# Decoder-step MLP on one core: PSUM split three ways, product order, early factors, and DMA issue moved to GpSimd

## The chip, the cores and the metric

The kernel runs on one core of one Trainium2 chip. The metric is the device time of one execution in microseconds; the time of a kernel is the median of its runs.

## The reference

One layer of a decoder trunk on 1024 prompt tokens and 8 sample tokens, width 1024, all float32: a pooling mixer and gated linear attention, cross-attention into 256 memory tokens, an MLP of hidden width 4096, and a final RMSNorm. The change touches the MLP and what surrounds it:

```python
hf = _rmsnorm(x, norm_ffn_g)
a = jax.nn.relu(jnp.einsum('btd,df->btf', hf, w_up))      # 1024 -> 4096
x = x + jnp.einsum('btf,fd->btd', a * a, w_down)          # 4096 -> 1024
y = _rmsnorm(x, norm_final_g)
```

## The kernel before, in words

**Arithmetic.** Every float32 operand of a large product is split into a high and a low part of the matmul type, and three partial products are summed: high by high, high by low, low by high. A split is a cast on ScalarE (L157) and a subtraction on VectorE (L158). Both MLP products use a two-by-two scheme with seven products in place of eight, numbered "1" to "7". Tokens are cut into columns 0 to 511 (HA = 512) and 512 to 1031 (HB = 520).

**The up product** comes in three pieces. The attention part ends with `run(ATTN)` (L1184) and the remaining columns of the attention's output projection (`add_ctx`, L1004). Then `first_products(m)` (L1114) runs for m = 0 to 15: products "1" and "2", 12 matmuls of 512 columns each, whose activated sum (tile `c11`) is stored to `fd["2"][m]` in HBM. Then `other_products(m)` (L1127) runs for m = 0 to 15. I call one m of it a row. A row loads four weight blocks into one slot `w4` (L1131), combines them on VectorE (L1140 to L1143), reloads the row's `c11` as `b11` (L1135), and runs products "4", "6", "5", "7", "3" in this order through `product` (L1107): "4" is 12 matmuls of 512 columns, each other one 24 of 260. Product "7" goes on accumulating in the accumulator of "6", and "3" in that of "5". So VectorE must have read "6" (L1155) before "7" starts, and ScalarE must have read "5" (L1158) before "3" starts. After that come the sums L1160 to L1164, the squared ReLU (L1111, L1112), and five factors formed by VectorE (L1172 to L1181; three of them are written over `w4`) and stored to HBM by GpSimd (L1173 to L1182). One more is stored by ScalarE (L1169).

**The down product** goes through the numbers in the order "2", "3", "1", "6", "5", "4", "7". For each it loads eight factors of two hidden blocks (`factor`, L1239, load at L1243, then split), and for each of four output blocks two weight pieces (`down_w`, L1248, load at L1257), multiplies (`down_part`, L1275), and adds to the residual blocks `X`, which `x2_load` (L1321, load at L1326) brings from HBM. The factors of the next number are loaded while the present one is multiplied.

**Buffers.** `S` (L66) has 19 slots of about 8 KB per partition, one for any `slot(...)`. During the rows they hold the split operands of products "3" to "7" (two slots each, ten in all), `P1` (four slots, each of four rows; one comes free after rows 3, 7, 11 and 15), the `w4` of the rows under way, and the early factors "2" (one slot each, kept until the down product). `tmp` (L68) has four buffers; a row takes two (`c12` with `b11`, and `c2`), a factor's raw load one. PSUM has eight banks: pool `mp` with two accumulators of one bank, `accp` with two of three banks (NG = 3). The down product opens pools of its own, with two of one bank and three of two banks.

**Order of the work.** The framework's scheduler puts the instructions of each engine in order ahead of time by the program's order and by when it expects operands and buffers; on the chip each engine, and each engine's DMA issue queue, then goes strictly in that order. A slot is taken when the DMA that read it last has landed. `first_factor` (L1201, load at L1206) is called after rows 2, 4, 5, 9 and 13; the remaining three factors "2" are loaded ahead of the down product's first weights, in program order. All loads of the MLP (L1131, L1135, L1206, L1243, L1257, L1326) are issued by SyncE (SP).

Of the kernel before, what the change touches and what calls it, by code (L numbers as in the profile page):

```python
# [8 lines left out]
F32 = mybir.dt.float32  # L9
# [51 lines left out]
def body(ctx, tc, a, o):  # L61
# [11 lines left out]
    mp = front.enter_context(tc.tile_pool(name="mp", bufs=2, space=PSUM))  # L73
    accp = front.enter_context(tc.tile_pool(name="accp", bufs=2, space=PSUM))
# [110 lines left out]
    def gemm_steps(src, X, name, cols=ALL):  # L185

        W = src if isinstance(src, list) else load_w(src, name)
        acc = accp.tile([P, NG, 512], F32, tag="acc", name="acc")
        yield acc[:, :len(cols), :cols[0][1] - cols[0][0]]
        for k in range(len(W)):  # L190
            hi, lo = W[k]
            for i, (w, j) in enumerate(((hi, 0), (hi, 1), (lo, 0))):
                for g, (c0, c1) in enumerate(cols):
                    PE.matmul(acc[:, g, :c1 - c0], w, X[k][j][:, c0:c1],  # L194
                              start=(k == 0 and i == 0), stop=(k == len(W) - 1 and i == 2))
            yield
# [54 lines left out]
    def tokens_sum(ss, name):  # L251

        pt = accp.tile([P, NG, 512], F32, tag="acc", name="pts")
# [102 lines left out]
    def x_chunk(k):  # L356
        xT = T("xT")
        acc = accp.tile([P, NG, 512], F32, tag="acc", name="ptx")
# [20 lines left out]
    def f_part(k):  # L379
        if k == 0:  # L380
            FW.append(accp.tile([P, NG, 512], F32, tag="acc", name="accf"))
        for j in range(2):
            for g in range(NG):
                PE.matmul(FW[KC][:, g, :GS], FW[k], H[k][j][:, g * GS:(g + 1) * GS],
                          start=(k == 0 and j == 0), stop=(k == KC - 1 and j == 1))
# [70 lines left out]
    def forget():  # L456
# [3 lines left out]
        for p in range(2):  # L460
            acc = accp.tile([P, NG, 512], F32, tag="acc", name="accz")
# [57 lines left out]
    def pool_out(gi):  # L519
# [6 lines left out]
        acc = accp.tile([P, NG, 512], F32, tag="acc", name="accp")  # L526
# [119 lines left out]
    def gla1(c):  # L646
        cs = slice(c * P, (c + 1) * P)
        acc = GA[c] = accp.tile([P, NG, 512], F32, tag="acc", name="accg")
# [297 lines left out]
    def scores(h, tt):  # L946
        acc = accp.tile([P, NG, 512], F32, tag="acc", name="accsc")
# [22 lines left out]
    def context(h, tt):  # L970
        pT = PT.pop((h, tt))
        acc = accp.tile([P, NG, 512], F32, tag="acc", name="accpv")
# [53 lines left out]
    def norm(half):  # L1026
# [3 lines left out]
        pt = accp.tile([P, NG, 512], F32, tag="acc", name="pts3")  # L1030
# [83 lines left out]
    def first_products(m):  # L1114
        acc = accp.tile([P, NG, 512], F32, tag="acc", name="acc12")
# [11 lines left out]
    def other_products(m):  # L1127
# [7 lines left out]
        SY.dma_start(b11[:, :HA], fd["2"][m])  # L1135
# [14 lines left out]

        d = mp.tile([P, 512], F32, tag="m", name="acc4")
        product([(d, 0, HA)], w_split(w4[:, 3]), "4")
        va, ta = both(accp.tile([P, NG, 512], F32, tag="acc", name="acc67"))
        product(ta, w_split(w4[:, 0]), "6")
        V.tensor_tensor(out=g2(c12), in0=va, in1=g2(p1), op=ALU.add)  # L1155
        vc, tc_ = both(accp.tile([P, NG, 512], F32, tag="acc", name="acc53"))
        product(tc_, w_split(s1), "5")
        A.copy(out=g2(c22), in_=vc)  # L1158
# [25 lines left out]
    run(ATTN)  # L1184
    for half in range(2):
# [15 lines left out]
    def first_factor(j):  # L1201

        ff = slot([P, 2, 2, HA], F32R, "F2")
        for k in range(2):
            t = wp.tile([P, HA], F32, tag="raw", name="fac2", bufs=3)
            SY.dma_start(t, fd["2"][2 * j + k])  # L1206
# [3 lines left out]
    for m in range(MU):  # L1210
        other_products(m)
        if m in (2, 4, 5, 9, 13):
            first_factor(len(F.get("2", [])))
# [9 lines left out]
    mp = ctx.enter_context(tc.tile_pool(name="mpd", bufs=2, space=PSUM, reuse_waits="tile"))  # L1223
    accp = ctx.enter_context(tc.tile_pool(name="accpd", bufs=3, space=PSUM, reuse_waits="tile"))
# [14 lines left out]
    def factor(n, j):  # L1239
# [3 lines left out]
        SY.dma_start(t, fd[n][2 * j:2 * j + 2].rearrange("k p n -> p k n"))  # L1243
# [77 lines left out]
    def x2_load(i, j, m):  # L1321
# [4 lines left out]
        SY.dma_start(X[i, j][:, m, :TH[j].stop - TH[j].start], xd[i * MD_ + m][:, TH[j]])  # L1326

    while len(F["2"]) < MU // 2:
        factor("2", len(F["2"]))

    for d, (n, blocks, op, outs) in enumerate(DOWN[:-1]):
        nxt = DOWN[d + 1][0]
        todo = list(range(MU // 2))
        for m in range(MD_):
# [3 lines left out]
            for q in range(2):  # L1338
                down_part(to, n, down_w(n, blocks, op, m, q), q)
# [100 lines left out]
```

## Time and profile before

| | |
|---|---|
| median of 3 runs | 1406.67 us (1399.91 to 1414.76) |
| profiled execution, its own time | 1404.68 us |
| its span, first to last instruction | 1403.0 us |
| TensorE busy | 95% of the span |
| VectorE, ScalarE, GpSimd busy | 65%, 41%, 16% |
| mean granted TensorE clock | 0.982 |
| up product, first_products | 706.9 to 802.4 us |
| up product, 16 rows of other_products | 802.4 to 1051.4 us |
| down product and end | 1051.4 to 1403.0 us |

The execution's own time lies 1.7 us above its span. The profile shows one execution; PE is TensorE's matmuls, PEld its weight loads, DVE VectorE, ACT ScalarE, POOL GpSimd, SPq SyncE's issue queue. "A <- B" means that A sat idle until B was done. Idle time of an engine off the critical path costs nothing by itself.

### The profile page before, as it was taken

The page shows a single profiled execution, that of the slowest core. Times are in us where ns is not written, and L with a number is a line of the kernel's source. Part 1 is how long each engine was busy: PE and PEld are TensorE (multiplying, and loading weights), DVE is VectorE, ACT ScalarE, POOL GpSimd, SP SyncE. Part 2 cuts the span into 40 slices and gives each one's busy share as a digit, 9 for nine tenths or more (in the row PEclk, how much of TensorE's full clock was granted, in tenths as well). Part 3 has the DMA queues.
Part 4 walks back from the last instruction along what each step waited for, and adds up shares of the span by engine and source line. Part 5 has one row for each costly group of instructions (what it writes and reads, how often), then busy time and mean ns, then how long its engine had stood idle before and what let it go on. Part 6 is the DMA issues. An engine that isn't in the chain of part 4 may idle for free. (4 is left out here: it accounts for less than half of the span.)

```text
span 1403.0 us, 22658 instructions
## 1 busy us (share of the span) xinstructions
PE 1331.8 (95%) x8734; PEld 1237.0 (88%) x8734; DVE 913.4 (65%) x1443; ACT 580.6 (41%) x1065; POOL 218.4 (16%) x229
## 2 busy tenths in 40 slices
PE   6999999899999989999999999998998999999996
PEld 6999999789999978878977799898986899999886
DVE  5776655886555577853768577677776654675663
ACT  6531122444345333533557445444445432342522
POOL 2143100331023022442200011112110000000000
PEclk9999999999999999999999999999998999999998
DMA  8846542674465436555435556555649955986671
GB/s 267 258 121 190 151 151 83 195 223 164 148 203 160 142 117 208 170 198 175 130 118 164 169 180 206 174 189 175 210 167 368 312 187 160 288 252 188 219 211 61
DMA packets 287557, 261.39 MB, mean 186 GB/s; under 512 B 13496, under 2 KB 239682, under 8 KB 287321
## 3 DMA queue, kind: packets, MB, share of 16 engines
q1 hardware_dynamic: 275289, 226.08, 52.0%
q0 software_dynamic: 6400, 21.17, 4.1%
q10 hardware_dynamic: 5760, 12.68, 2.5%
q8 instruction: 69, 1.13, 0.3%
q14 instruction: 39, 0.32, 0.1%
HBM read 195.04 MB, written 64.85 MB: 185 GB/s over the span
## 5 line engine op out<-in xcount | busy, mean ns | idle before, releaser
L1107 PE MATMUL acc<-T,wuph 128*128 128x260 f32 (+1 forms) x1408 | 288.6, 317 | 13.0 <-DVE c L1155 9.2
L1275 PE MATMUL accd<-F,wdnh 128*128 128x260 f32 (+1 forms) x1344 | 266.3, 310 | 6.1 <-ACT wdnh L157 6.1
L1107 PEld LDWEIGHTS acc<-T,wuph 128*128 128x128 f32 x1408 | 214.4, 191 | 33.8 <-ACT c L1158 5.2
L1275 PEld LDWEIGHTS accd<-F,wdnh 128*128 128x128 f32 x1344 | 201.1, 189 | 20.2 <-ACT wdnh L157 6.3
L1107 PE MATMUL acc<-T,wupl 128*128 128x260 f32 (+1 forms) x704 | 180.6, 317 | 3.6 <-DVE wupl L158 3.6
L1275 PE MATMUL accd<-F,wdnl 128*128 128x260 f32 (+1 forms) x672 | 167.4, 311 | 2.8 <-DVE wdnl L158 2.7
L1107 PEld LDWEIGHTS acc<-T,wupl 128*128 128x128 f32 x704 | 116.8, 191 | 13.1 <-DVE wupl L158 4.8
L1275 PEld LDWEIGHTS accd<-F,wdnl 128*128 128x128 f32 x672 | 109.5, 189 | 11.7 <-DVE wdnl L158 4.7
L157 ACT CAST wdnh<-wdn 128x1024 fp32r<-128x1024 f32 x52 | 54.8, 1053 | 129.8 <-PE accd L1275 124.2
L157 ACT CAST F<-fac 128x1040 fp32r<-128x1040 f32 (+2 forms) x61 | 59.9, 986 | 63.0 <-DMA fac<-fd 49.9
L158 DVE TENSOR_TENSOR F<-fac,F 128x1040 fp32r<-128x1040 f32 (+2 forms) x61 | 68.9, 1143 | 18.6 <-ACT F L157 18.0
L194 PE MATMUL acc<-c,womh 128*128 128x260 f32 (+2 forms) x384 | 80.8, 321 | 0.0
L158 DVE TENSOR_TENSOR wdnl<-wdn,wdnh 128x1024 fp32r<-128x1024 f32 x52 | 63.5, 1221 | 23.6 <-ACT wdnh L157 23.6
L194 PE MATMUL acc<-hm,wqmh 128*128 128x344 f32 x384 | 74.6, 328 | 0.0
L157 ACT CAST wuph<-w 128x512 fp32r<-128x512 f32 x64 | 38.6, 617 | 67.5 <-PE acc L1107 65.2
L194 PEld LDWEIGHTS acc<-c,womh 128*128 128x128 f32 x384 | 59.4, 188 | 6.4 <-ACT womh L157 0.8
L194 PEld LDWEIGHTS acc<-hm,wqmh 128*128 128x128 f32 x384 | 63.3, 192 | 0.6
L1111 ACT ACTIVATE c<-c 128x512 f32<-128x512 f32 (+1 forms) x64 | 40.2, 636 | 55.2 <-DVE c L1161 24.9
L158 POOL TENSOR_TENSOR vs<-vt,vs 128x512 fp32r<-128x512 f32 x32 | 47.3, 1506 | 95.2 <-ACT vs L157 91.7
L1259 DVE TENSOR_TENSOR wdn<-wdn 128x1024 f32<-128x1024 f32 x24 | 29.4, 1225 | 41.8 <-DMA wdn<-in_w_down 41.8
L194 PE MATMUL acc<-c,woml 128*128 128x260 f32 (+2 forms) x192 | 49.7, 320 | 0.0
L158 DVE TENSOR_TENSOR wupl<-w,wuph 128x512 fp32r<-128x512 f32 x64 | 42.7, 686 | 4.5 <-ACT wuph L157 4.4
(402 smaller groups left out, 2620.4 us busy)
## 6 DMA issues: line engine op xcount, KB each, us to landing
wdn<-in_w_down SPq DMA_DIRECT2D x64, 512.0 KB
fac<-fd SPq DMA_DIRECT2D x32, 520.0 KB
w<-in_w_up SPq DMA_DIRECT2D x64, 256.0 KB
ws<-in_w_down SPq DMA_DIRECT2D x48, 256.0 KB
fac<-fd SPq DMA_DIRECT2D x19, 512.0 KB
fd<-w POOLq DMA_DIRECT2D x32, 260.0 KB, 2.6
x<-xd SPq DMA_DIRECT2D x16, 516.0 KB
xd<-x SPq DMA_DIRECT2D x16, 516.0 KB
```

The lines of the kernel that those rows point to most:

```text
L157: A.copy(out=dst_hi, in_=src)
L158: (eng or V).tensor_tensor(out=dst_lo, in0=src, in1=f(dst_hi), op=ALU.subtract)
L194: PE.matmul(acc[:, g, :c1 - c0], w, X[k][j][:, c0:c1], start=(k == 0 and i == 0), stop=(k == len(W) - 1 and i == 2))
L1107: PE.matmul(acc, w, t[k // 2][:, k % 2, j, c0:c1], start=(first and k == 0 and i == 0), stop=(k == HK - 1 and i == 2), skip_group_check=True)
L1111: A.activation(out=t, in_=t, func=AF.Relu)
L1259: V.tensor_tensor(out=raw[0], in0=raw[0], in1=raw[1], op=op)
L1275: PE.matmul(acc, W[x][:, k, :], ff[:, y, k % 2, c0:c1], start=(q == 0 and k == 0 and i == 0), stop=(q == 1 and k == UK - 1 and i == 2))
```

## The change

PSUM: the front part's two PSUM pools are closed after the attention schedule, and the down product's pools (two accumulators of one bank, three of two banks) are opened there, so that they serve the rest of `add_ctx`, `norm`, the up product and the down product. A name BANKS (3 before that point, 2 after it) replaces NG in every allocation from `accp`. In a row the order of the products becomes "6", "5", "4", "7", "3". Early factors are taken after rows 5, 9 and 13 only, so five factors "2" are left to the down product instead of three. The loads L1135, L1206, L1243 and L1326 are issued by GpSimd. The first two weight pieces of the down product are requested ahead of the remaining factors "2".

```diff
-    mp = front.enter_context(tc.tile_pool(name="mp", bufs=2, space=PSUM))
-    accp = front.enter_context(tc.tile_pool(name="accp", bufs=2, space=PSUM))
+    front_p = ctx.enter_context(ExitStack())
+    mp = front_p.enter_context(tc.tile_pool(name="mp", bufs=2, space=PSUM))
+    accp = front_p.enter_context(tc.tile_pool(name="accp", bufs=2, space=PSUM))
+    BANKS = NG
...
     def other_products(m):
...
-        SY.dma_start(b11[:, :HA], fd["2"][m])
+        G.dma_start(b11[:, :HA], fd["2"][m])
...
+        va, ta = both(accp.tile([P, BANKS, 512], F32, tag="acc", name="acc67"))
+        product(ta, w_split(w4[:, 0]), "6")
+        V.tensor_tensor(out=g2(c12), in0=va, in1=g2(p1), op=ALU.add)
+        vc, tc_ = both(accp.tile([P, BANKS, 512], F32, tag="acc", name="acc53"))
+        product(tc_, w_split(s1), "5")
+        A.copy(out=g2(c22), in_=vc)
         d = mp.tile([P, 512], F32, tag="m", name="acc4")
         product([(d, 0, HA)], w_split(w4[:, 3]), "4")
-        va, ta = both(accp.tile([P, NG, 512], F32, tag="acc", name="acc67"))
-        product(ta, w_split(w4[:, 0]), "6")
-        V.tensor_tensor(out=g2(c12), in0=va, in1=g2(p1), op=ALU.add)
-        vc, tc_ = both(accp.tile([P, NG, 512], F32, tag="acc", name="acc53"))
-        product(tc_, w_split(s1), "5")
-        A.copy(out=g2(c22), in_=vc)
         product(ta, w_split(w4[:, 2]), "7", first=False)
...
     run(ATTN)
+    front_p.close()
+    mp = ctx.enter_context(tc.tile_pool(name="mpd", bufs=2, space=PSUM, reuse_waits="tile"))
+    accp = ctx.enter_context(tc.tile_pool(name="accpd", bufs=3, space=PSUM, reuse_waits="tile"))
+    BANKS = 2
...
-            SY.dma_start(t, fd["2"][2 * j + k])
+            G.dma_start(t, fd["2"][2 * j + k])
...
-        if m in (2, 4, 5, 9, 13):
+        if m in (5, 9, 13):
             first_factor(len(F.get("2", [])))
...
-    mp = ctx.enter_context(tc.tile_pool(name="mpd", bufs=2, space=PSUM, reuse_waits="tile"))
-    accp = ctx.enter_context(tc.tile_pool(name="accpd", bufs=3, space=PSUM, reuse_waits="tile"))
...
-        SY.dma_start(t, fd[n][2 * j:2 * j + 2].rearrange("k p n -> p k n"))
+        G.dma_start(t, fd[n][2 * j:2 * j + 2].rearrange("k p n -> p k n"))
...
-        SY.dma_start(X[i, j][:, m, :TH[j].stop - TH[j].start], xd[i * MD_ + m][:, TH[j]])
-
+        G.dma_start(X[i, j][:, m, :TH[j].stop - TH[j].start], xd[i * MD_ + m][:, TH[j]])
+
+    W = [down_w("2", None, None, 0, q) for q in range(2)]
     while len(F["2"]) < MU // 2:
         factor("2", len(F["2"]))
...
-                down_part(to, n, down_w(n, blocks, op, m, q), q)
+                down_part(to, n, W.pop(0) if W else down_w(n, blocks, op, m, q), q)
```

## Rows read from the trace of the kernel before

**Rows 1.** First part of the profile page: busy time by engine, share, instructions.

```profile
PE 1331.8 (95%) x8734; PEld 1237.0 (88%) x8734; DVE 913.4 (65%) x1443; ACT 580.6 (41%) x1065; POOL 218.4 (16%) x229
```

**Rows 2.** Windows: length, busy PE, PEld, DVE, ACT, POOL, granted clock, DMA share, GB/s.

```profile
706.90:743.00 36.10, 32.72 (x138) 25.08 (x136) 28.26 (x47) 22.58 (x39) 0.00 (x0) 1.00 0.38 116
...
802.40:1051.40 249.00, 235.82 (x1729) 225.44 (x1727) 188.95 (x304) 113.58 (x198) 42.41 (x90) 0.98 0.57 188
1051.40:1059.90 8.50, 1.22 (x2) 0.50 (x2) 7.62 (x10) 5.79 (x8) 2.85 (x6) 0.68 0.85 239
1059.90:1106.40 46.50, 46.47 (x192) 37.48 (x193) 27.85 (x26) 21.10 (x21) 0.00 (x0) 0.95 0.99 350
...
1180.00:1260.00 80.00, 78.46 (x647) 77.54 (x646) 53.92 (x50) 31.09 (x30) 0.00 (x0) 1.00 0.85 252
```

**Rows 3.** Busy time by window, line 1107 alone (PE, PEld, clock, DMA): one row.

```profile
816.68:830.95 14.27, 14.27 (x110) 13.75 (x109) 1.00 0.51 172
```

**Rows 4.** Waits of PE, 802.4 to 1051.4: total, times, longest.

```profile
PE acc L1107 <- DVE c L1155: 9.2, 7, 1.8
```

**Rows 5.** Waits of DVE in the same window.

```profile
DVE s L1140 <- DMA w<-in_w_up: 31.6, 13, 3.7
```

**Rows 6.** Waits of SP's issue queue in the same window.

```profile
SPq L1131 <- DMA fd<-w: 132.5, 17, 13.8
```

**Rows 7.** Timeline of SP, first weight load of two successive rows: start, length.

```profile
904.46 0.37 SPq L1131 DMA_DIRECT2D w<-in_w_up  x1
...
920.09 0.37 SPq L1131 DMA_DIRECT2D w<-in_w_up  x1
```

**Rows 8.** Chain that ended last, same stretch: the last of the four weight loads.

```profile
906.58 4.80 DMA w<-in_w_up
```

**Rows 9.** Timeline of DVE, same stretch; in brackets the idle time before.

```profile
911.47 0.69 DVE L1140 TENSOR_TENSOR s<-w 128x512 f32<-128x512 f32 x1 [1.44 <-DMA w<-in_w_up]
...
916.42 0.69 DVE L1179 TENSOR_TENSOR w<-c,c 128x520 f32<-128x520 f32 x1
...
918.25 0.69 DVE L1155 TENSOR_TENSOR c<-acc,p 128x520 f32<-128x520 f32 x1
```

**Rows 10.** Timeline of POOL, same stretch: the last store out of a `w4`.

```profile
917.41 0.54 POOL L1180 DMA_DIRECT2D fd<-w  x1
```

**Rows 11.** DMA issues of the page: queue, count, size, median us to landing.

```profile
fd<-w POOLq DMA_DIRECT2D x32, 260.0 KB, 2.6
```

**Rows 12.** Waits of PE, 706 to 746: total, times, longest.

```profile
PE acc L1107 <- DVE c L1123: 1.3, 2, 0.9
```

**Rows 13.** Timeline of PE from the up to the down product.

```profile
1057.45 1.22 PE L1275 MATMUL accd<-F,wdnh 128*128 128x512 f32 x2 [6.07 <-ACT wdnh L157]
1059.93 0.79 PE L1275 MATMUL accd<-F,wdnl 128*128 128x512 f32 x1 [1.26 <-DVE wdnl L158]
```

**Rows 14.** Timeline of SP in that stretch.

```profile
1043.02 8.56 SPq L1243 DMA_DIRECT2D fac<-fd  x3
1051.63 0.46 SPq L1257 DMA_DIRECT2D wdn<-wsd  x1
1055.13 0.36 SPq L1243 DMA_DIRECT2D fac<-fd  x1
```

**Rows 15.** Timeline of ACT in that stretch: the cast of the first down weights.

```profile
1056.36 1.04 ACT L157 CAST wdnh<-wdn 128x1024 fp32r<-128x1024 f32 x1
```

**Rows 16.** Timeline of DVE in that stretch: the split of the last factor "2".

```profile
1056.92 1.22 DVE L158 TENSOR_TENSOR F<-fac,F 128x1024 fp32r<-128x1024 f32 x1
```

**Rows 17.** Timeline of POOL in that stretch: the last store of row 15.

```profile
1059.04 0.54 POOL L1182 DMA_DIRECT2D fd<-c  x1 [1.07 <-DVE c L1181]
```

**Rows 18.** Timeline of SP: the first load of an early factor.

```profile
805.95 0.34 SPq L1206 DMA_DIRECT2D fac<-fd  x1
```

**Rows 19.** Chain that ended last, down product: the longest factor load in it.

```profile
1200.09 6.77 DMA fac<-fd
```

More of the change, by code (lines that the diff above doesn't have):

```diff
@@ L187, in gemm_steps @@
         W = src if isinstance(src, list) else load_w(src, name)
-        acc = accp.tile([P, NG, 512], F32, tag="acc", name="acc")
+        acc = accp.tile([P, BANKS, 512], F32, tag="acc", name="acc")
         yield acc[:, :len(cols), :cols[0][1] - cols[0][0]]
@@ L251, in tokens_sum @@
     def tokens_sum(ss, name):
-        pt = accp.tile([P, NG, 512], F32, tag="acc", name="pts")
+        pt = accp.tile([P, BANKS, 512], F32, tag="acc", name="pts")
         for g in range(NG):
@@ L357, in x_chunk @@
         xT = T("xT")
-        acc = accp.tile([P, NG, 512], F32, tag="acc", name="ptx")
+        acc = accp.tile([P, BANKS, 512], F32, tag="acc", name="ptx")
         for t in range(NCH):
@@ L380, in f_part @@
         if k == 0:
-            FW.append(accp.tile([P, NG, 512], F32, tag="acc", name="accf"))
+            FW.append(accp.tile([P, BANKS, 512], F32, tag="acc", name="accf"))
         for j in range(2):
@@ L460, in forget @@
         for p in range(2):
-            acc = accp.tile([P, NG, 512], F32, tag="acc", name="accz")
+            acc = accp.tile([P, BANKS, 512], F32, tag="acc", name="accz")
             for g in range(NG):
@@ L525, in pool_out @@
         w2 = wpool[gi]
-        acc = accp.tile([P, NG, 512], F32, tag="acc", name="accp")
+        acc = accp.tile([P, BANKS, 512], F32, tag="acc", name="accp")
         for q, (x, y) in enumerate(((0, 0), (0, 1), (1, 0))):
@@ L647, in gla1 @@
         cs = slice(c * P, (c + 1) * P)
-        acc = GA[c] = accp.tile([P, NG, 512], F32, tag="acc", name="accg")
+        acc = GA[c] = accp.tile([P, BANKS, 512], F32, tag="acc", name="accg")
         qz = qzs[c % 2]
@@ L946, in scores @@
     def scores(h, tt):
-        acc = accp.tile([P, NG, 512], F32, tag="acc", name="accsc")
+        acc = accp.tile([P, BANKS, 512], F32, tag="acc", name="accsc")
         av = acc[:, :2, :].rearrange("p x (y n) -> p (x y) n", y=2)
@@ L971, in context @@
         pT = PT.pop((h, tt))
-        acc = accp.tile([P, NG, 512], F32, tag="acc", name="accpv")
+        acc = accp.tile([P, BANKS, 512], F32, tag="acc", name="accpv")
         for j in range(2):
@@ L1029, in norm @@
             r3.append(sm.tile([P, NT], F32, tag="rbc", name="r3", bufs=1))
-        pt = accp.tile([P, NG, 512], F32, tag="acc", name="pts3")
+        pt = accp.tile([P, BANKS, 512], F32, tag="acc", name="pts3")
         cols = HALVES[half]
@@ L1114, in first_products @@
     def first_products(m):
-        acc = accp.tile([P, NG, 512], F32, tag="acc", name="acc12")
+        acc = accp.tile([P, BANKS, 512], F32, tag="acc", name="acc12")
         product([(acc[:, 0, :HA], 0, HA)], load_w(w_up_block(0, 0, m), "wup"), "1")
```

## The prediction

> **What bounds the kernel now.** I read the page's busy times first: TensorE (PE) is busy 95% of the span, every other engine 65% or less [rows 1]. So the change can only win what PE loses by standing still or by running at a lower granted clock, and the next view is where that happens. The windows [rows 2] show it: the sixteen rows of the up product have PE busy for 235.82 of 249.0 us at a clock of 0.98, and the 8.5 us between up and down product have it busy for 1.22 us. The windows of the down product are nearly full: 46.47 of 46.5, 78.46 of 80.
>
> A row that isn't disturbed takes 14.27 us, PE busy throughout [rows 3]; sixteen take 16 x 14.27 = 228.3 us. The rows took 249.0, so 20.7 us are lost: 249.0 - 235.82 = 13.2 us idle and 7.5 us in matmuls at the lower of the two clock levels, 1.2 instead of 2.4 GHz, which the rows show behind some of the idle spells.
>
> The waits of PE put most of the idle time, 9.2 us in 7 spells, on L1155, the read of product "6" that "7" waits for [rows 4]. L1155 needs nothing late itself; it sits in VectorE's queue. VectorE's only long wait is L1140 for the row's weights, 31.6 us in 13 spells [rows 5], and those weights are late because SP waited 132.5 us in all for stores out of older `w4` slots [rows 6]. Read in order of time this is a ring. The first load of a row is issued at 904.46 [rows 7]; the fourth one, issued by 906.58, lands 4.80 us later at 911.38 [rows 8]; L1140 starts at 911.47 and, ten instructions later in the same queue, L1179 writes the last factor over an older `w4`, 916.42 to 917.11 [rows 9]; its store is issued at 917.41 [rows 10] and lands 2.6 us later [rows 11], near 920.0; the next row's first load goes out at 920.09 [rows 7]. One turn is 920.09 - 904.46 = 15.63 us, and the mean row is 249.0 / 16 = 15.56. The rows run at the pace of this ring and not of PE. L1155 comes behind L1179 in that queue, at 918.25 [rows 9], which is how the ring reaches PE.
>
> **The change part by part.**
>
> *Fewer early factors.* From row 5 on the 19 slots of `S` held ten operand slots, three of `P1` and three early factors, which leaves three `w4`; later each `P1` that goes is replaced by a factor. Without the calls after rows 2 and 4 it is five. A load that waited for the store of three rows before now waits for the store of five rows before: it can be issued two rows (28.5 us) sooner, against a need of at most 3.7 us (the longest spell in rows 5). The ring then spans three rows with 15.63 us, 5.2 a row, and PE's 14.27 binds. VectorE's work fits: 188.95 / 16 = 11.8 us a row [rows 2], 83% of 14.27. Gain between 0 (the slots go to something else) and 20.7 us; I take 20, since undisturbed rows stand in the trace as they are.
>
> *Order of the products.* "4" between "5" and "7" gives L1155 and the read of "5" one more product, about a fifth of 14.27 = 2.9 us. While the ring binds, this moves the stall and doesn't remove it; without the ring there is nothing to cover. The first row now needs combined weights for its first product where "4" took a plain block: two subtractions of 0.69 us [rows 9]. Between a loss of 1.4 and no gain beyond the 20.7 above; I take 0.
>
> *Three accumulators of two banks.* Of PE's 13.2 idle us in the rows 9.2 fall on L1155 and the other 4.0 on splits of weights, none on the readers that free an accumulator (L1160, L1164). In `first_products` 1.3 us do fall on a reader of `acc`, L1123 [rows 12], in a window where PE is busy for 32.72 of 36.10 us [rows 2]. Gain 0 to 3.4 (all of that idle time), and a pool that opens in mid-program can cost a wait for the old accumulators of the same size; I take 1.
>
> *`b11` by GpSimd.* Sixteen issues at 0.54 us each (a store's row, rows 10) on a queue that works 42.41 of 249.0 us [rows 2], against one fewer between SP's weight loads. A row's first and last weight load lie 906.58 - 904.46 = 2.1 us apart with this load between them; at most a fifth of that is won per turn, and only while the ring binds. What queues behind the load on GpSimd are the stores of the next row, which come some 9 us later. I take 0, between a gain of 1 and a loss of 1.
>
> *From up to down.* PE starts at 1057.45 after 6.07 us of waiting for the weights' cast, stops again 1.26 us for their low part [rows 13], and then runs at a clock of 0.95 for the 46.5 us of product "2" [rows 2]. Its 192 matmuls at the full clock would be 46.5 x 0.95 = 44.2 us (0.23 each); from PE's end at 1057.45 - 6.07 = 1051.38 to 1106.40 it took 55.0, so 10.8 us are lost. The first weights were issued at 1051.63, right behind the third of three factor loads that had waited for buffers since 1043.02 [rows 14], and cast at 1056.36 [rows 15]. With weights alone on SP and requested first, that goes: I take a start 1.5 us after the last product (a cast of 1.04 and a hop). What is late next are factors, five instead of three. Their raw loads share two `tmp` buffers until row 15 has stored its sums; the old pace was four loads from 1043.02 to 1055.13, the third issued at 1051.2 (the three end at 1051.58) [rows 14], one in 4.0 us, so a fifth goes out near 1059.2. The third was split by 1058.14 [rows 16], 6.9 us after its issue, so the fifth is ready near 1066.1, 14.7 us past PE's end. PE, started 1.5 us past and using a factor per six matmuls (1.4 us), wants the eighth 1.5 + 7 x 1.4 = 11.3 past: a wait of 3.4. With 1.3 us of slow clock that is 6.2 lost, a gain of 4.6. Bounds: all but the start is won (9.3), or 4.2 more is lost (the second rival).
>
> The Trainium skill, "DMA: Bandwidth & Descriptors", section "Issuing engines are not separate DMA queues", says that DMAs of all issuers run on the same sixteen engines and a second issuer saves only issue time. By that rule this edit would be worth three issues of 0.4 us, and the total would come to 1382.5. The trace shows another cost, an issue queue that stands still for a buffer with weights behind it [rows 14], which the rule doesn't count.
>
> *The rest of the down product.* Factor and residual loads move from SP to GpSimd, 0.36 to 0.54 us an issue. PE lost 80.0 - 78.46 = 1.5 us in its worst window [rows 2], so at most 1.5 is won. DMA engines are 0.99 and 0.85 busy there; 1 MB of factors comes on top near 1060 (1 MB at 350 GB/s is 3 us), and product "2" has 17 us of slack in bytes (eight weight pieces and eight factors of some 0.5 MB and 2 MB of residual, at 350 GB/s 30 us of 46.5). I take 0, between a gain of 1.5 and a loss of 8 (a tenth of such a window).
>
> **The sum.** 1404.7 (the profiled execution) - 20 - 1 - 4.6 = 1379.1. The median of the runs lies 2.0 above that execution; I forecast 1380, and for this outcome 1370 to 1388.
>
> **The rivals.**
>
> *The ring stays.* The scheduler fixes who gets a slot ahead of time, and it may give the two free ones to factors or hold loads in their old places; then the change does not do what it says in the rows. For it: in the old trace the first early factor, called after row 2, was loaded at 805.95, in row 0 [rows 18], so what the scheduler does isn't what the calls say. Against: row 1, still with more slots, ran in 14.27 us [rows 3]. Only accumulators and transition count: 1404.7 - 5.6 = 1399.
>
> *Factors late.* GpSimd's queue goes in order, and the last store of row 15 leaves it only at 1059.04, 7.7 us past PE's end [rows 17]. If the fourth and fifth factors stand behind it, the fourth is ready near 7.7 + 6.9 = 14.6 past and the fifth, in the buffer of one before, near 21 to 23, some 11 us after PE wants it. The transition then loses 1.5 + 11 + 2.5 of slow clock = 15 instead of 10.8: 1404.7 - 21 + 4.2 = 1388.
>
> *Slower: one factor at a time.* If GpSimd's loads don't overlap one another, each takes up to 6.77 us, the longest in the old chain [rows 19], and eight per product take 54.2 against 44.2 us of PE for a product (one of 512 columns); six lose 10 each at most, some 54 in all. Time 1404.7 - 21 + 54 = 1438. It decides from 44.2 / 8 = 5.5 us a load. Against: stores of half that size on the same queue are issued 0.6 us apart and land in 2.6 [rows 11], so they overlap.
>
> The Trainium skill, "SBUF — State Buffer", section "SBUF: two separate sides", warns that GpSimd can't write descriptors while VectorE runs an operation in a two-port mode; by that rule loads could get this slow. VectorE's rows here are operations on two tensors [rows 9], which the page doesn't count among them.
>
> **How the numbers follow.** Forecast 0.62, factors late 0.15, ring stays 0.13, slower 0.05, something better or other 0.05. The range from 1368 to 1397 leaves out the ring that stays, the slower case and part of the rest, about 0.2. A measurement of this kernel tells about 1% (14 us) from no change: faster than 1392.6 are the forecast, most of the second rival and part of the rest, 0.79; within 1% 0.16; slower 0.05.
>
> **What would show it.** Right: rows of 14.3 us throughout, no wait of L1140 for weights, SP's loads two rows ahead, the first down matmul within 3 us of the last up matmul, and a wait there on a factor's split. Wrong: rows still at 15.6 with SP waiting for stores; or the wait between up and down as long as before, on the DMA of factors; or new waits for factors in products "3" to "5".

## The result: 0.9% slower, and the profile after

The changed kernel takes 1420.27 us (median of 15 runs, 1413.04 to 1425.59) against 1407.87 us of the kernel before in the same session: a ratio of 1.0087, interval 1.0067 to 1.0107. I had predicted 1380 with a range up to 1397. The step is smaller than the 1% that I had called "same", but it goes the wrong way, and 40 us lie between forecast and result.

I cut both profiled executions at the same four events: first and last matmul of the up product, first matmul of the down product, first matmul of product "3", first of product "4". Columns are the stretch, its length, busy time of PE, PEld, DVE, ACT, POOL with instruction counts, the granted clock, the DMA engines' share and GB/s. Before:

```profile
706.90:1051.40 344.50, 327.91 (x2118) 297.24 (x2116) 253.61 (x408) 172.72 (x301) 42.77 (x93) 0.99 0.55 176
1051.40:1057.50 6.10, 0.05 (x1) 0.05 (x1) 5.24 (x8) 5.79 (x8) 1.83 (x4) 0.75 0.84 260
1057.50:1106.20 48.70, 47.44 (x192) 37.77 (x193) 30.23 (x29) 20.90 (x20) 1.02 (x3) 0.93 0.98 342
1106.20:1293.10 186.90, 185.36 (x1538) 184.40 (x1538) 109.64 (x106) 64.61 (x63) 0.12 (x1) 1.00 0.75 231
```

After:

```profile
709.10:1053.50 344.40, 330.37 (x2118) 296.58 (x2116) 251.90 (x403) 169.07 (x297) 56.97 (x118) 0.98 0.56 179
1053.50:1058.90 5.40, 0.06 (x2) 0.04 (x1) 4.56 (x7) 4.68 (x9) 1.84 (x4) 0.88 0.78 247
1058.90:1106.50 47.60, 46.60 (x193) 37.39 (x194) 32.93 (x32) 23.23 (x23) 20.45 (x34) 0.94 1.01 353
1106.50:1309.20 202.70, 189.11 (x1538) 187.55 (x1537) 109.73 (x106) 64.04 (x63) 22.18 (x33) 0.97 0.70 210
```

Two things are to be seen. The up product, where I expected 20 us, gained 0.1. And products "3", "1", "6", "5", where I expected nothing, lost 15.8 us: 13.6 us of idle PE instead of 1.5, and a clock of 0.97 instead of 1.00. Gap and product "2" together gained 1.8.

**The rows.** VectorE's waits of the changed kernel from the first row to the end of the up product (us in all, times, longest):

```profile
DVE s L1142 <- DMA w<-in_w_up: 18.0, 8, 4.7
DVE F L160 <- ACT F L159: 13.5, 3, 4.9
```

PE's largest wait in the rows:

```profile
PE acc L1109 <- DVE c L1155: 5.8, 3, 2.4
```

L1142 is what L1140 was in [rows 5]: the sum `s1`, the first reader of a row's weights. It still waits for loads. Of PE's ten idle spells in the rows, 11.1 us in all, nine (10.5 us) come within 8 us behind such a wait; the waits for casts of factors (L160) have one of 0.6 us behind them. One such wait in VectorE's queue (start, duration, operation, idle time before it):

```profile
894.17 0.69 DVE L1164 TENSOR_TENSOR c<-c,acc 128x512 f32<-128x512 f32 x1
898.28 0.69 DVE L1142 TENSOR_TENSOR s<-w 128x512 f32<-128x512 f32 x1 [3.43 <-DMA w<-in_w_up]
898.90 0.69 DVE L1166 TENSOR_TENSOR c<-acc,c 128x520 f32<-128x520 f32 x1
...
903.13 0.69 DVE L1155 TENSOR_TENSOR c<-acc,p 128x520 f32<-128x520 f32 x1
```

```profile
903.97 1.20 PE L1109 MATMUL acc<-T,wuph 128*128 128x260 f32 x4 [2.41 <-DVE c L1155]
```

The load it waits for went out at 891.57. It is row 9's load while row 5 is being summed, and PE comes to row 9 only some 40 us later (rows of about 14.3 us). But L1166 and, eight places on, L1155 of row 6 stand behind `s1`, and PE waits for L1155. The shape is that of [rows 8, 9]; only the distance has grown.

**The down product.** The longest spell of PE lies near 1260. GpSimd's factor loads, SP's weights, then VectorE and PE, each with its idle time and what ended it:

```profile
1247.84 0.72 POOL L1247 DMA_DIRECT2D fac<-fd  x1 [33.88 <-DVE F L160]
1248.98 0.71 POOL L1247 DMA_DIRECT2D fac<-fd  x1 [0.42 <-DVE F L160]
1250.10 0.72 POOL L1247 DMA_DIRECT2D fac<-fd  x1 [0.42 <-DVE F L160]
...
1257.47 0.71 POOL L1247 DMA_DIRECT2D fac<-fd  x1 [1.16 <-DVE F L160]
```

```profile
1250.97 1.50 SPq L1261 DMA_DIRECT2D wdn<-in_w_down  x2
```

```profile
1264.36 1.23 DVE L1263 TENSOR_TENSOR wdn<-wdn 128x1024 f32<-128x1024 f32 x1 [6.59 <-DMA wdn<-in_w_down]
1251.00 0.51 PE L1279 MATMUL accd<-F,wdnl 128*128 128x260 f32 x2 [1.65 <-DVE wdnl L160]
1259.11 1.24 PE L1279 MATMUL accd<-F,wdnh 128*128 128x260 f32 x4 [2.56 <-ACT wdnh L159]
1266.78 0.80 PE L1279 MATMUL accd<-F,wdnl 128*128 128x260 f32 x2 [6.44 <-DVE wdnl L160]
```

Six factor loads of 512 KB start in 10 us. They are factors of product "4", which starts at 1309.2. The weights of 1250.97, which PE needs next, are read at 1264.36, 13.4 us after the first of the two was issued. The three PE spells shown are 10.7 of the stretch's 13.6 us of idle time.

### The profile page after: what moved, and what is told of

Its sections match the earlier page's. It is cut to its first block, busy times and chain, and to the rows that moved or that the text cites. A ratio compares the mean times of both kernels' runs of the same rounds, so it can differ in the third digit from the quotient of the medians.

```text
span 1420.1 us, 22668 instructions
## 1 busy us (share of the span) xinstructions
PE 1337.7 (94%) x8734; PEld 1239.9 (87%) x8734; DVE 916.0 (64%) x1441; ACT 577.1 (41%) x1063; POOL 276.8 (19%) x320
## 4 chain that ended last, share of the span: by engine, by line
PE 53%; DMA 16%; DVE 15%; issue 9%; ACT 4%; SPq 1%; POOL 1%; DVEq 0%; ACTq 0%; POOLq 0%
PE acc L196 27%; PE acc L1109 11%; PE accd L1279 6%; DMA wdn<-in_w_down 6%; DMA fac<-fd 3%; DMA w<-in_w_up 2%; DVE kt L858 2%; DVE wdn L1263 1%; DMA kt<-in_cache_mem_k 1%; DVE F L160 1%; DMA qb<-qdr 1%; PE accv L732 1%; PE accl L1279 1%; PE acck L345 1%; SPq L1133 1%
## 5 line engine op out<-in xcount | busy, mean ns | idle before, releaser
L160 DVE TENSOR_TENSOR F<-fac,F 128x1040 fp32r<-128x1040 f32 (+2 forms) x59 | 68.4, 1175 | 35.4 <-ACT F L159 35.2
L1247 POOL DMA_DIRECT2D fac<-fd x53 | 37.9, 715 | 219.8 <-DVE F L160 179.4
L160 DVE TENSOR_TENSOR wdnl<-wdn,wdnh 128x1024 fp32r<-128x1024 f32 x52 | 63.3, 1219 | 22.2 <-ACT wdnh L159 22.2
L160 POOL TENSOR_TENSOR vs<-vt,vs 128x512 fp32r<-128x512 f32 x32 | 47.4, 1510 | 93.5 <-ACT vs L159 90.6
L1263 DVE TENSOR_TENSOR wdn<-wdn 128x1024 f32<-128x1024 f32 x24 | 29.4, 1223 | 47.1 <-DMA wdn<-in_w_down 47.0
L160 DVE TENSOR_TENSOR wupl<-w,wuph 128x512 fp32r<-128x512 f32 x64 | 43.3, 685 | 12.9 <-ACT wuph L159 12.6
```

The costliest lines, as they stand in the source:

```text
L160: (eng or V).tensor_tensor(out=dst_lo, in0=src, in1=f(dst_hi), op=ALU.subtract)
L1247: G.dma_start(t, fd[n][2 * j:2 * j + 2].rearrange("k p n -> p k n"))
L1263: V.tensor_tensor(out=raw[0], in0=raw[0], in1=raw[1], op=op)
```

## The experiments

The table gives each run's median, its ratio to the kernel before in the same session with the interval, and four stretches of its profiled execution (up product; gap; product "2"; products "3" to "5"), cut as above. One execution's start of the up product varies by up to 7 us (706.3 to 713.5) with the same program ahead of it, so stretches are compared, not positions. A stretch varies too: changed, fac_sync, weights_pool and swap_queues are written alike up to the down product and took 341.5 to 344.4 us for the up product, and s1_late and both, alike as well, 343.8 and 337.3. So differences of some 3 to 6 us in one stretch of one execution prove nothing by themselves. The runs are referred to by the names in the first column.

| run | us | ratio | up | gap | "2" | "3"–"5" |
|---|---|---|---|---|---|---|
| before | 1407.9 | 1 | 344.5 | 6.1 | 48.7 | 186.9 |
| changed | 1420.3 | 1.0087 [1.0067, 1.0107] | 344.4 | 5.4 | 47.6 | 202.7 |
| fac_sync | 1410.8 | 1.0026 [1.0007, 1.0044] | 341.5 | 5.8 | 55.1 | 187.3 |
| before_fac_pool | 1432.5 | 1.0167 [1.0130, 1.0204] | 342.6 | 8.2 | 49.2 | 205.4 |
| weights_pool | 1422.2 | 1.0103 [1.0063, 1.0143] | 343.7 | 6.4 | 53.1 | 197.0 |
| swap_queues | 1439.6 | 1.0213 [1.0175, 1.0250] | 342.7 | 7.9 | 57.8 | 200.7 |
| fewer_early | 1395.5 | 0.9910 [0.9877, 0.9942] | 324.0 | 6.1 | 55.7 | 189.9 |
| psum_order | 1404.3 | 0.9976 [0.9953, 0.9999] | 338.9 | 5.8 | 48.0 | 187.0 |
| order_fewer_early | 1403.0 | 0.9959 [0.9935, 0.9984] | 339.8 | 5.7 | 50.2 | 186.5 |
| order_only | 1401.5 | 0.9951 [0.9930, 0.9971] | 336.3 | 7.6 | 49.3 | 189.3 |
| psum_only | 1392.9 | 0.9889 [0.9866, 0.9912] | 323.4 | 6.4 | 55.0 | 187.1 |
| b11_pool | 1396.0 | 0.9920 [0.9885, 0.9955] | 328.3 | 6.7 | 50.9 | 188.9 |
| early_pool | 1399.5 | 0.9936 [0.9910, 0.9962] | 332.7 | 6.5 | 50.1 | 189.8 |
| s1_late | 1420.3 | 1.0098 [1.0064, 1.0132] | 343.8 | 5.7 | 49.2 | 202.3 |
| both | 1407.7 | 0.9979 [0.9956, 1.0001] | 337.3 | 4.9 | 54.2 | 187.2 |
| s1_late_fac_sync | 1402.7 | 0.9969 [0.9946, 0.9992] | 331.7 | 7.1 | 54.3 | 188.9 |
| five_early | 1398.9 | 0.9934 [0.9909, 0.9959] | 331.3 | 4.7 | 54.6 | 187.0 |
| before_s1_late | 1394.3 | 0.9920 [0.9891, 0.9950] | 329.4 | 6.7 | 48.6 | 186.5 |
| s1_late_first_row | 1394.4 | 0.9905 [0.9877, 0.9934] | 326.7 | 6.1 | 48.4 | 188.8 |
| weights_first | 1393.7 | 0.9899 [0.9870, 0.9928] | 327.8 | 4.8 | 48.9 | 189.2 |

### The down product: who issues the factors

fac_sync, the changed kernel with one line back:

```diff
-        G.dma_start(t, fd[n][2 * j:2 * j + 2].rearrange("k p n -> p k n"))
+        SY.dma_start(t, fd[n][2 * j:2 * j + 2].rearrange("k p n -> p k n"))
```

Expected: 

> The changed kernel with one line back: the down product's factor loads are issued by SyncE again, behind and between its weights. Theory A (burst): on their own queue the factor loads go out six at a time as soon as buffers allow, the weights issued in the same stretch share the DMA engines with them and land 12 us after issue instead of 5, and TensorE waits. Then the stretch from the first down matmul to the last full-width one shrinks from 320 us to about 304, the 10 us gaps near 1256 to 1267 go, and the time falls by 14 to 16 us to about 1405. Rival B (the new loss in the down product comes from something else: residual loads on GpSimd, the new pools, fewer early factors): the stretch stays at 315 to 320 us and the time within 4 us of the changed kernel's.

Measured 1410.8, and 187.3 us for products "3" to "5": all 15 us are back there. Product "2" took 7.5 us of it again (47.6 to 55.1), where PE stands a second time, 4.1 us, for the cast of a weight. before_fac_pool is the reverse, the same line moved to GpSimd in the kernel before.

Expected: 

> The old kernel with one line changed: the down product's factor loads alone are issued by GpSimd. Theory A: this line alone makes the down product 10 to 16 us longer, near 1420. Rival B: within 4 us of the old kernel's 1407.

Measured 1432.5: one line costs 24.7 us, 18.5 of them in products "3" to "5". That stretch in fac_sync and in before_fac_pool:

```profile
1110.70:1298.00 187.30, 185.12 (x1538) 184.43 (x1537) 108.69 (x105) 62.77 (x62) 2.25 (x5) 1.00 0.72 224
1113.40:1318.80 205.40, 190.19 (x1537) 188.64 (x1536) 109.06 (x106) 62.68 (x62) 20.02 (x29) 0.96 0.68 205
```

So the issuer of the factors is the whole loss of that stretch, in either kernel.

Where the time goes is seen in the DMA queues (q0 carries what GpSimd issues, q1 what SP issues). The first two lines are the changed kernel from 1250.9 to 1264.4, while the late weights were under way; the third is fac_sync at the corresponding place, 1249.4 to 1262 (queue, packets, MB, share of the sixteen engines):

```profile
q0 software_dynamic: 795, 2.87, 65.1%
q1 hardware_dynamic: 2080, 1.05, 29.4%
```

```profile
q1 hardware_dynamic: 4844, 3.64, 95.2%
```

The engines move 291 GB/s in both. On one queue a weight asked for at 1250.54, with two factor loads issued right behind it, is read at 1256.58. On two, factors that are wanted 50 us later take two thirds of the engines and the weights get 1.05 MB in 13.5 us. My reading is that one queue serves first what was issued first; the rows show the delays and the shares, not the order of the packets. The Trainium skill, "DMA: Bandwidth & Descriptors", section "Queues, rings and completion order", says that a DMA engine takes turns between the queues that have work, a packet from each. These rows agree in that both queues advance at once; the turns themselves are not in the trace.

Two runs tried to separate "two queues" from "GpSimd's queue". weights_pool puts the down weights on GpSimd too:

```diff
-            SY.dma_start(raw[-1], src)
+            G.dma_start(raw[-1], src)
```

Expected: 

> The changed kernel with the down product's weights issued by GpSimd as well, so that weights and factors stand in one queue in the order of the program. Theory (order: on a queue of their own six factor loads go out in a burst and the weights that are wanted first land among them, 12 us after their issue): one queue sets the order again, weights land within 7 us, 1408 to 1413, as with the factors on SyncE (1410.8). Rival (GpSimd's queue itself is slower per transfer): no better than the changed kernel, 1418 to 1430, with weights landing 10 us or more after their issue.

swap_queues has the weights on GpSimd and the factors on SP.

Expected: 

> The changed kernel with the two queues of the down product exchanged: weights issued by GpSimd, factors by SyncE. Theory (two queues share the DMA engines, so that loads wanted later hold up those wanted now, whichever queue has which): products of width 260 take 197 us or more where one queue on SyncE took 187, 1415 to 1425. Rival (only a factor load on GpSimd is harmful, as it runs ahead in bursts): 187 to 190 us there, 1406 to 1411.

weights_pool missed its 1408 to 1413: 1422.2. Its weights land in 5.4 us in the median and 9.0 at most, so the load of 13 us is gone. Yet products "3" to "5" take 197.0, ten more than in fac_sync, where the same loads stand in one queue on SP, and PE waits there for weights again (8.9 us in six spells). One difference is in its issue rows: a weight occupies GpSimd 0.88 us, where SP's issue of one takes 0.37. Its queue also stands still for buffers with factors behind it (rows below), but so does SP's in fac_sync (83.2 us on the same reader). Why GpSimd's one queue loses is not shown.

```profile
1251.91 0.88 POOL L1261 DMA_DIRECT2D wdn<-in_w_down  x1 [3.84 <-DVE wdn L1263]
1253.07 0.70 POOL L1247 DMA_DIRECT2D fac<-fd  x1 [0.27 <-DVE F L160]
```

swap_queues came out slower than its own theory, 1439.6, with 200.7 there and 57.8 in product "2". Sharing is seen in the changed kernel's rows, but these two show that weights on GpSimd lose by themselves as well. How much of swap_queues is which, stays open. So it is shown that the issuer of the factors costs the 15 us; that the lost order is the reason is seen in one place, and one queue on GpSimd did not win it back.

### The rows: which part takes the gain away

fewer_early is the kernel before with one edit, the prediction's main step by itself:

```diff
-        if m in (2, 4, 5, 9, 13):
+        if m in (5, 9, 13):
```

Expected: 

> The kernel before with the early factors after rows 5, 9 and 13 only, nothing else. My prediction's step: two more slots for w4 let each load go out two rows sooner, the ring is gone, rows of 14.3 us: 1385 to 1390 with five factors to load between up and down product. Rival (the scheduler puts s1's sum behind the new load, as many rows ahead as slots allow, so VectorE goes on waiting for loads just issued): rows still lose 15 to 22 us in fewer, longer spells, 1402 to 1412.

The up product took 324.0 us instead of 344.5, with PE busy for 320.56 of them, and L1140 waited for a load once:

```profile
707.70:1031.70 324.00, 320.56 (x2118) 291.78 (x2116) 254.87 (x404) 170.06 (x297) 42.64 (x93) 1.00 0.58 184
```

```profile
DVE s L1140 <- DMA w<-in_w_up: 0.3, 1, 0.3
```

The step and its size, 20 us, were right. The time fell by 11.7 only: product "2" takes 55.7 instead of 48.7 and the next ones 189.9 instead of 186.9. In product "2" PE stands a second time, 3.0 us at 1056.98, for a weight load that ScalarE's cast waits for, and the granted clock stays down longer: 0.83 from 17 to 37 us into the product, where the kernel before is back at 1.00. That five factors are left is not enough to explain it: order_only, with five left too, takes 49.3.

So another part of the change undoes it. order_fewer_early adds the order "6", "5", "4", "7" and the accumulators:

Expected: 

> The kernel before with the order 6, 5, 4, 7, the three accumulators and the three early factors together; all loads stay on SyncE and down weights in their old place. In the old order three early factors alone made all sixteen rows run at 14.3 us (1395.5), in the changed kernel they did not (22 us lost), though VectorE's queue holds s1 just as many rows ahead in both. Theory G (the loads given to GpSimd, b11 and the early factors, spoil the rows): rows undisturbed here, 1392 to 1397. Theory O (the order of the products does: product 5 comes second and needs s1 two products sooner): rows lose 12 us or more, 1402 to 1410.

order_only and psum_only add one of the two. The order's edit:

```diff
-        d = mp.tile([P, 512], F32, tag="m", name="acc4")
-        product([(d, 0, HA)], w_split(w4[:, 3]), "4")
...
         A.copy(out=g2(c22), in_=vc)
+        d = mp.tile([P, 512], F32, tag="m", name="acc4")
+        product([(d, 0, HA)], w_split(w4[:, 3]), "4")
```

Expected (order_only): 

> The kernel before with three early factors and the new order of a row's products, the accumulators as before. With order and accumulators together the rows lost 16 us (244.2 us instead of 228.5 with three early factors alone). If the order does it: rows 240 to 246 us again, 1401 to 1406. If the accumulators do: rows near 229, 1394 to 1398.

Expected (psum_only): 

> The kernel before with three early factors and the three accumulators of two banks, the products in their old order. If the order does it: rows near 229 us, 1393 to 1397, at or below the fastest so far (1393.7). If the accumulators do: rows 240 to 246, 1401 to 1406.

The order does it: up product 336.3 with the order, 323.4 with the accumulators, 339.8 with both. The up product of order_only and of psum_only, and then L1140 in order_only, and L1142 in psum_only, over the rows:

```profile
706.30:1042.60 336.30, 324.88 (x2118) 292.66 (x2116) 252.24 (x403) 169.47 (x296) 42.63 (x93) 1.00 0.56 177
713.50:1036.90 323.40, 320.74 (x2118) 291.88 (x2116) 254.46 (x404) 169.87 (x298) 42.64 (x93) 1.00 0.58 184
```

```profile
DVE s L1140 <- DMA w<-in_w_up: 12.1, 9, 3.0
```

```profile
DVE s L1142 <- DMA w<-in_w_up: 2.4, 2, 1.4
```

In the medians the order costs less, as product "2" gives some of it back (55.7 to 49.3 and 55.0 to 50.2): 1395.5 to 1401.5 alone, barely clear of the noise, and 1392.9 to 1403.0 beside the accumulators.

What remains (339.8 to 344.4, within what one stretch varies) I looked for in GpSimd's loads. early_pool is fewer_early with `b11` and the early factors loaded by GpSimd, b11_pool with `b11` alone.

Expected (early_pool): 

> The other half: the kernel before with three early factors, in the old order, with b11 and the early factors loaded by GpSimd. Theory G: the casts of early factors stand in ScalarE's queue for loads that GpSimd issues behind stores, rows lose 8 to 20 us, 1402 to 1412. Theory O: rows of 14.3 us as with the same loads on SyncE, 1393 to 1398.

Expected (b11_pool): 

> The same with only b11 on GpSimd and the early factors on SyncE. If G holds by the early factors alone: 1393 to 1398, rows undisturbed. If by b11: 1402 to 1412. If O holds: 1393 to 1398 too.

Up product 332.7 and 328.3 instead of 324.0: 4.3 us for `b11`, 4.4 for the early factors, both in one execution each; in the medians (1399.5 and 1396.0 against 1395.5) neither can be told from nothing. The trace of early_pool does show a wait: L1140 stands 8.1 us for loads in five spells, and PE's three waits on L1155 (5.7 us) each come behind one of them, in the rows where early factors are cast.

psum_order has the order and the accumulators with the old five early factors:

Expected: 

> The kernel before with the order of the products (6, 5, 4, 7) and the three accumulators of two banks, nothing else: early factors, queues and first down weights as before. My prediction: a gain of 1 (0 to 3.4), 1404 to 1408. Rival: as the stall of the rows comes from VectorE's queue, the other order only moves it, and the first row starts later because its first product needs combined weights: 1408 to 1412.

It took 1404.3, with 338.9 us for the up product. Where the ring still binds, order and accumulators together cost nothing that shows, as the prediction said. Beside order_fewer_early (1403.0, 339.8) it shows one thing more: in the new order the two slots that fewer early factors leave gain nothing.

### The reader's place in the queue

The waits of L1142 (or L1140) have one shape: it stands in VectorE's queue ahead of work that PE needs, and waits for a load issued 5 to 7 us earlier. If that is the mechanism, keeping `s1` out of the queue until later must help without touching slots. The edit gives `s1` the buffer `u3`, which is free only when the row before has been summed:

```diff
-        s1 = wp.tile([P, HK, P], F32, tag="raw", name="s1", bufs=3)
+        s1 = u3[:, :HK * P].rearrange("p (k n) -> p k n", k=HK)
```

The edit also takes `s1` out of the three buffers that it shares with the raw loads of the early factors; no run separates this from the later place. In the kernel before (before_s1_late), with its five early factors and three slots for `w4`:

Expected: 

> The kernel before with one edit: s1 in u3's buffer, which is free only after the row before has been summed, so that the scheduler can't place the sum that reads the new weights two rows ahead in VectorE's queue. Ring by slots (my prediction): the same loads wait for the same stores, 1405 to 1410, L1140 still waits 20 us or more for weights in the rows. Ring by the reader's place in VectorE's queue: most of those waits go, rows near 14.3 us, less a first row that starts 3 to 5 us late: 1390 to 1398.

Measured 1394.3, 12.6 us faster by one line, and no wait of L1140 for a weight load is left in the rows. 22.9 us of VectorE's idle time now stand ahead of it, 4.4 of them until a store out of its new buffer has landed and 18.5 for which the profile names no releaser, while PE has work (it stands 3.3 us in all there):

```profile
DVE c L1140 <- issue: 18.5, 8, 3.8
DVE c L1140 <- DMA fd<-c: 4.4, 4, 2.1
```

In the old order the ring of the prediction therefore needs both halves, few slots and a reader that stands ahead in the queue, and it is enough to remove one. In the new order more slots alone did not remove the waits (18.0 us in the changed kernel).

In the changed kernel (s1_late) the same line gave nothing in time.

Expected: 

> The changed kernel with one line changed: the sum s1 of two weight blocks is written into the row's own tile u3 instead of a rotating buffer, so VectorE's queue can hold it no earlier than one row ahead of its use (before this it stands three to four rows ahead, right behind the load that fills it). Theory C (the ring stays because VectorE's queue has the first reader of each newly requested weight load directly behind the store that frees its slot): the sixteen rows shrink from 251 us to about 230 (14.3 a row), VectorE's waits for weight loads go from 18 us to under 3, and the time falls by 15 to 20 us. Rival D (rows are held up by the early factors' loads on GpSimd, whose casts ScalarE waits for, or by VectorE's total work): the rows stay above 245 us and the time within 5 us.

Most rows ran in 14.3 us. In the first one PE waited 3.5 us for the cast of combined weights; the row near 910, behind the cast of an early factor, lost 3; and the row near 1000 lost 6, where `s1` waited 7.25 us, to 1001.48, for a store out of its new buffer. That row's stores by GpSimd landed 6.7 to 7.7 us after issue, where the page's median is 2.6: four down weights of 512 KB, wanted only from 1058 on, had gone out between 988.7 and 994.2. It looks like the spell of 1260, a transfer wanted now beside loads wanted late. With fac_sync's line too (both):

Expected: 

> Both edits of the two kernels before. A and C together: the gains add, about 30 to 35 us below the changed kernel, near 1385 to 1390, and below the old kernel's 1407 too. If A holds and C fails: near 1405. If they overlap (the rows' gain is given back at the start of the down product): 1395 or more.

1407.7, the kernel before again. s1_late_fac_sync moved the early factors back to SP and kept the first row's own buffer; five_early also went back to five early factors:

Expected (s1_late_fac_sync): 

> The changed kernel with s1 in u3's buffer (the first row excepted), and all factor loads, the early ones too, back on SyncE. Theory: what the rows still lost with s1 in u3 was the first row's wait for c2 (805.97 to 809.51, with 2 us of slow clock behind it) and the early factors, whose casts stand in ScalarE's queue ahead of the row's weights and wait for a load that GpSimd issues behind a store (912.78 to 917.02). Both go: some 5 + 5 us under the kernel with both edits (1407.7), 1395 to 1400, rows of 14.3 us nearly throughout. Rival: the cast's place in ScalarE's queue is what costs, whichever queue issues the load; then only the first row gains: 1402 to 1405, with the spell in the row of the early factor still there.

Expected (five_early): 

> The same as the kernel before it in this set (s1 in u3, all factor loads on SyncE), but with the five early factors of the old kernel, after rows 2, 4, 5, 9 and 13. Theory A (my prediction's ring: three slots for w4 hold the rows at 15.6 us each): the rows lose up to 20 us again, 1410 to 1415. Theory B (the place of the first reader of a load in VectorE's queue sets the pace, the number of slots doesn't, once s1 is late): rows as in the run with three early factors, and two factors fewer to load between up and down product, so the gap of 4.4 us on a factor's cast goes: 1390 to 1397.

1402.7 and 1398.9. The first missed its 1395 to 1400: PE still stands twice, 2.7 us in all, between 906.3 and 909.8, behind the cast of the second early factor (901.51), and then runs at the lower clock from about 911 to 914.5 (four matmuls take 1.07 us there and 0.64 before and after). The second shows that with `s1` late the number of slots doesn't matter: 331.3 us for the up product with five early factors against 331.7 with three. Why product "2" still takes 54.6 us there, with three factors left, isn't settled.

On the side of the kernel before, the first row's own buffer (s1_late_first_row) and the weights requested first (weights_first):

Expected: 

> The kernel before with s1 in u3's buffer in all rows but the first, which keeps its own buffer. With s1 in u3 in every row (1394.3) the only loss left in the rows was the first one's: 2.1 us of standing still (808.88 to 810.99) and 1.8 us of slow clock. If that wait was for u3 of the row before the first, it goes: 1390 to 1392. Rival: the first row waits for its weights anyway, 1394 as with the line in all rows.

Expected: 

> The kernel with s1 late in all rows but the first (first of this set), and the down product's first two weights requested ahead of its factors, all on SyncE. My prediction's step: PE starts sooner after the up product and nothing is lost behind it, 3 to 5 us under the first of this set. Rival: the start comes 1 to 3 us sooner, but the factors that stand behind the weights come later in product 2 (49 us became 54 to 55 in the runs with weights first and factors on SyncE), so the sum is the same or 1 to 4 us slower.

1394.4 and 1393.7: neither differs from before_s1_late by more than the runs can tell. With the weights first the gap is 4.8 instead of 6.1 us, and product "2" 48.9 instead of 48.4.

The fastest are psum_only, weights_first, before_s1_late and s1_late_first_row, 1392.9 to 1394.4, about 1% under the kernel before and not told apart among themselves, nor from fewer_early (1395.5). All four keep the old order and all loads on SP.

## Why the prediction was wrong, point by point

**The ring in the rows (right by itself).** In the old order "the ring then spans three rows" and the 20 us hold: fewer_early gained 20.5 in the up product. The reading of [rows 4 to 11] was sound but for two slips on which nothing hangs: L1179 stands eight instructions behind L1140, not ten, and L1140's wait is VectorE's only long one for a load, while L1160 waits 21.2 us for PE.

**"Order of the products ... I take 0" (the step that failed in the rows).** I bounded it between a loss of 1.4 and no gain, arguing that without the ring there is nothing to cover. Measured with three early factors, the order costs 336.3 - 324.0 = 12.3 us of the up product alone and 339.8 - 323.4 = 16.4 beside the accumulators, and with it the two free slots gain nothing (338.9 with five early factors, 339.8 with three): most of the 20 us went with the order. I priced the two subtractions of one row and the cover of "5" and "7", and not that a new order makes a new queue on VectorE. Row 9 shows it. In fewer_early its `s1` runs at 895.86, 7 us behind the last sum of row 5 (888.99), its loads all issued by 885.4; in the changed kernel it runs at 898.28, right ahead of that sum (898.90), its loads issued from 891.57 to 893.6. Over the rows `s1` waits 0.3 us for loads in fewer_early, 12.1 in order_only and 18.0 in the changed kernel. That the scheduler expected the load sooner there is my reading; no run shows its estimates.

**"`b11` by GpSimd ... 0" and the early factors on GpSimd.** Together some 4 us in the medians (1399.5 against 1395.5), not clear of the noise. I had no price at all for the early factors' issue. VectorE waited 13.5 us in three spells for casts of factors in the changed kernel, but those spells have next to nothing on PE behind them (0.6 us).

**Three accumulators, gain 1.** 324.0 to 323.4 in the up product, 1395.5 to 1392.9 in the medians: a gain of 1 can't be told from none here.

**From up to down, gain 4.6.** Measured 54.8 - 53.0 = 1.8 over gap and product "2". "I take a start 1.5 us after the last product" failed: PE's first matmul came 5.3 us after the up product's last one. The weights' loads had gone out by 1024.7, but their cast stands in ScalarE's queue behind two factor casts that wait for loads and behind row 15's squared ReLU (changed kernel, ScalarE's queue):

```profile
1049.92 1.05 ACT L159 CAST F<-fac 128x1024 fp32r<-128x1024 f32 x1 [4.03 <-DMA fac<-fd]
1052.64 1.05 ACT L159 CAST F<-fac 128x1024 fp32r<-128x1024 f32 x1 [1.68 <-DMA fac<-fd]
...
1057.78 1.03 ACT L159 CAST wdnh<-wdn 128x1024 fp32r<-128x1024 f32 x1
```

I had taken the wait for the weights' DMA out of the sum and not asked what is late next in the queue of the engine that casts them. The wait for a late factor that I did price didn't come in the changed kernel; with the factors on SP it did (4.4 us on a factor's cast in both). Weights requested first, by themselves, gained 0.8 over gap and product "2" (weights_first against s1_late_first_row), less than can be told.

**"The rest of the down product ... I take 0, between a gain of 1.5 and a loss of 8" (the step that failed in the down product).** It lost 15.8. I compared bytes with bandwidth over a whole product, in which there is slack, and took a queue for a cost of issue only. By the rows near 1260, what SP's one queue also did was order: weights issued ahead of factors were read 6 us after issue there, and 13.4 us with the factors in a queue of their own. That this is the whole reason is not shown, since weights_pool, with one queue on GpSimd, still lost ten of the fifteen. My slower rival had the place (factors on GpSimd) and the wrong mechanism, factors that don't overlap: six went out within 10 us and moved 2.87 MB in 13.5 us. My sign of being wrong, new waits for factors, looked at the wrong load: PE waited for weights. The Trainium skill, "DMA: Bandwidth & Descriptors", section "Issuing engines are not separate DMA queues", says that transfers of all issuers run on the same sixteen engines and that a second issuer saves only issue time; the prediction had 1382.5 by it. The traces agree with the first (65.1% and 29.4% of the sixteen engines in one spell); the second leaves out this loss.

**The sum.** 1379.1 + 20.9 (the up product gained 0.1 and not 20 + 1) + 2.8 (4.6 - 1.8 in the transition) + 15.8 (products "3" to "5") = 1418.6, where the profiled execution took 1421.8; 2.2 of the rest is the later start of the up product (709.1 and not 706.9), in a part of the program that is the same.

## What to carry to other kernels

When loads move to a second queue, count what the first queue did as an order, not only its issue time: bulk loads that are wanted late can take the engines from those wanted now, as they did near 1260 here. When operations are reordered or buffers added under a scheduler that fixes queues ahead of time, look where the first reader of each early load comes to stand, since one early reader in a queue that goes in order holds all behind it; tying that reader to a buffer that comes free late is a one-line remedy (12.6 us in the kernel before, nothing in the changed one). And try each part of a change alone: here one part was worth 11.7 us and others ate it and more.

## What the runs showed of the hardware

The same weights and factors travel in other packets by the other issuer. From 1100 to 1300 us, fac_sync's hardware queue took 53164 packets for 42.65 MB, 0.8 KB each; weights_pool's software queue took 11955 for 43.54 MB, 3.6 KB each:

```profile
q1 hardware_dynamic: 53164, 42.65, 69.0%
```

```profile
q0 software_dynamic: 11955, 43.54, 70.2%
```

Larger packets moved no more bytes per share of the engines (0.62 MB per 1% in both), and weights_pool's stretch was the slower one all the same.
